# Queueing the last load of v one unit sooner, and a GpSimd drain right after its last store

One core of one Trainium2 chip (trn2). The metric is the device time of one execution in microseconds (us), of which several are taken; the profile is of one execution, and its span starts and ends with the program's first and last instruction, so it is some 1.7 us shorter than the time.

## The reference

```python
attn_weights: float32 [8, 12, 1024, 1024]      v: float32 [8, 12, 1024, 64]
out = np.einsum('bhqs,bhsd->bhqd', attn_weights, v)          # float32
```

There are 96 heads. The kernel takes them two at a time, as 48 units (numbered 0 to 47). A unit's attention is 8 MB in HBM and is cast to bf16 on its way in; the loads of all units are nearly all of the kernel's traffic.

## The kernel before

GpSimd issues every transfer that casts (all attention, all v but the first), and every store but those of the last unit. It does so in one program order, and its transfers run through one queue, in that order. TensorE transposes a unit's attention in 16 groups (line 129), spreads v over the partitions (line 144, waits for v) and multiplies (line 172; in the last three units line 225, group by group). VectorE and ScalarE copy between.

The parts that matter, with cuts marked:

```python
HELD = 9                       # the last nine GpSimd stores wait until all loads are queued
pieces_of = {                  # unit -> pieces of its attention load, (first group, groups)
    NP - 4: [(0, GH), (GH, GH)],
    NP - 3: [(0, GH), (GH, GH)],
    NP - 2: [(0, 4), (4, 4), (8, 4), (12, 4)],
    NP - 1: [(0, 4), (4, 4), (8, 4), (12, 2), (14, 1), (15, 1)],
}
# ... TensorE, units 45 to 47
            transpose_g(abf[i], g)
            if g == 3:
                # ...
                elif p == NP - 2:
                    pe.wait_ge(s_vlast, 16)          # unit 46 needs the last v here
                spread_v(i, vr_of(p))
# ... GpSimd
HELD_FROM = NP - 1 - HELD
for p in range(NP - 2):
    pool.wait_ge(s_t[True], (p + 1) * PER_DVE)       # unit p is transposed: its buffer is free
    if p % 2 == 1 and (p + 1) // 2 < NV:
        iv = (p + 1) // 2
        if iv < NV - 1:
            pool.wait_ge(s_sp[1], p + 1)
        load_v(iv)                                   # iv == NV - 1 goes to vr_last
    load_attn(p + 2)
    if 0 < p <= HELD_FROM:
        store(p - 1)
for p in range(HELD_FROM, NP - 1):
    store(p)
# ... SyncE: the last unit's four stores as they become ready, then waits for all stores
```

`vr_last` is a buffer of its own, used by nothing else, so its load has nothing to wait for. A buffer of attention serves every second unit.

## Time and profile before

| | |
|---|---|
| time, median of 3 runs | 1068.31 us (1067.46 to 1068.49) |
| span of the profiled execution | 1066.0 us |
| loads and stores in GpSimd's queue | 128 |
| last attention piece landed | 1040.9 us |
| GpSimd's last store landed | 1052.2 us |
| last copy of a result by an engine | 1058.0 us |
| SyncE's last store landed | 1059.65 us |

A landing is read as the issue's start plus the latency that the profile gives for that transfer's tile. The page's "chain that ended last" ends with the last instruction of a compute engine; what lies between that and the end of the span (8 us here) is not in it and has to be read from the landings and from the sequencers' instructions. The lines themselves stand in the prediction.

### The profile page before, as it was taken

Reading aid. Unit: us, or ns where it says so; the run is one execution under the profiler, and the core shown is the slowest. Engines: PE = TensorE matmul, PEld = TensorE weight load, DVE = VectorE, ACT = ScalarE, POOL = GpSimd, SP = SyncE. Lnnn points to the kernel's source line nnn. Section 1 sums busy time; section 2 is a strip of 40 time slices with the busy share of each in tenths; the row PEclk is TensorE's granted clock in tenths of the full one; section 3 lists DMA queues with packets and bytes.
Section 4 is the critical chain, followed back from the end, with each engine's and each line's share of the span. In section 5 each row is a group of like instructions: output and inputs, shape, how many; then the busy total and the mean of one; then the engine's idle time right before and its main releaser. Section 6 shows DMA issues by size and latency. Waiting matters only on the chain.

```text
span 1066.0 us, 12832 instructions
## 1 busy us (share of the span) xinstructions
PE 792.5 (74%) x5640; PEld 635.4 (60%) x5640; DVE 391.8 (37%) x589; ACT 397.1 (37%) x485; POOL 71.1 (7%) x137
## 2 busy tenths in 40 slices
PE   0896686867877778768787787767876778769866
PEld 0764575646655666546665575556755566558755
DVE  0443353333433344334343343333433334335423
ACT  0343343333433334333343343333433334335423
POOL 1000000000000000000000000000000000001020
PEclk9898898888989789898888798987889889889979
DMA  9999999999999999999999999999999999999994
GB/s 216 217 217 219 242 225 230 223 229 237 223 231 222 236 230 223 230 231 227 230 224 221 243 223 231 222 229 239 221 231 221 236 232 221 218 215 216 212 217 189
DMA packets 19171, 239.84 MB, mean 225 GB/s; under 512 B 2128, under 2 KB 2512, under 8 KB 11984
## 3 DMA queue, kind: packets, MB, share of 16 engines
q0 software_dynamic: 18432, 238.03, 99.3%
q1 hardware_dynamic: 720, 1.57, 0.4%
q8 instruction: 9, 0.15, 0.0%
q14 instruction: 10, 0.08, 0.0%
HBM read 427.82 MB, written 25.17 MB: 425 GB/s over the span
## 4 chain that ended last, share of the span: by engine, by line
DMA 67%; PE 29%; issue 1%; POOL 1%; ACT 1%; DVE 0%; POOLq 0%; SPq 0%
DMA abf<-in_attn_weights_dram 66%; PE bank L129 23%; PE bank L144 2%; PE bank L225 2%; DMA vr_last<-in_v_dram 1%; POOL vr L387 1%; PE bank L172 1%; ACT at L320 0%; PE bank L156 0%; DVE vbf L295 0%; DVE at L320 0%; DVE osb L307 0%; ACT osb L347 0%; ACT vbf L295 0%; POOL abf L381 0%
## 5 line engine op out<-in xcount | busy, mean ns | idle before, releaser
L129 PE MATMUL bank<-ident,abf 128*128 128x128 f32 x3072 | 464.1, 322 | 251.0 <-DMA abf<-in_attn_weights_dram 251.0
L129 PEld LDWEIGHTS bank<-ident,abf 128*128 128x128 f32 x3072 | 452.1, 215 | 273.3 <-DMA abf<-in_attn_weights_dram 247.7
L320 DVE COPY at<-bank 128x1024 bf16<-128x1024 bf16 x480 | 320.6, 689 | 469.8 <-PE bank L129 465.1
L320 ACT COPY at<-bank 128x1024 bf16<-128x1024 bf16 x288 | 289.0, 1012 | 421.5 <-PE bank L129 421.4
L172 PE MATMUL bank<-at,vbf 128*64 128x512 bf16 x1440 | 216.4, 391 | 0.8 <-DVE vbf L295 0.8
L172 PEld LDWEIGHTS bank<-at,vbf 128*64 128x64 bf16 x1440 | 106.5, 108 | 96.1 <-DVE vbf L295 8.2
L357 ACT COPY ot<-bank 128x512 f32<-128x512 f32 x45 | 26.3, 585 | 183.7 <-PE bank L172 183.7
L357 DVE COPY ot<-bank 128x512 f32<-128x512 f32 x45 | 31.1, 692 | 144.4 <-PE bank L172 144.4
L381 POOL DMA_DIRECT2D abf<-in_attn_weights_dram x58 | 31.0, 539 | 398.2 <-PE bank L129 395.2
L156 PEld LDWEIGHTS bank<-ident,ot 128*128 128x128 f32 x360 | 38.5, 140 | 19.1 <-issue 19.1
L156 PE MATMUL bank<-ident,ot 128*128 128x128 f32 x360 | 49.1, 280 | 0.0
L347 ACT COPY osb<-bank 128x512 f32<-128x512 f32 x90 | 48.3, 589 | 0.4
L144 PE MATMUL bank<-vr,spread 32*128 32x512 bf16 x368 | 48.1, 377 | 0.0
L387 POOL DMA_DIRECT2D vr<-in_v_dram x22 | 11.6, 528 | 476.5 <-PE bank L144 476.5
L295 DVE CAST vbf<-bank 128x512 bf16<-128x512 f32 x48 | 33.2, 692 | 24.6 <-PE bank L144 24.6
L295 ACT CAST vbf<-bank 128x512 bf16<-128x512 f32 x48 | 28.1, 585 | 32.3 <-PE bank L144 32.3
L225 PE MATMUL bank<-vbf,at 128*128 128x128 bf16 x384 | 28.0, 227 | 4.3 <-DVE vbf L295 1.9
L397 POOL DMA_DIRECT2D out_dram<-osb x47 | 25.1, 543 | 70.9 <-ACT osb L347 48.3
L225 PEld LDWEIGHTS bank<-vbf,at 128*128 128x128 bf16 x384 | 24.4, 102 | 7.7 <-issue 3.2
L144 PEld LDWEIGHTS bank<-vr,spread 32*128 32x128 bf16 x368 | 15.4, 93 | 15.7
L307 DVE COPY osb<-bank 64x256 f32<-64x256 f32 (+1 forms) x13 | 5.1, 395 | 22.0 <-PE bank L225 22.0
L307 ACT COPY osb<-bank 64x256 f32<-64x256 f32 (+1 forms) x13 | 4.6, 351 | 22.1 <-PE bank L225 22.1
(13 smaller groups left out, 10.7 us busy)
## 6 DMA issues: line engine op xcount, KB each, us to landing
abf<-in_attn_weights_dram POOLq DMA_DIRECT2D x44, 4096.0 KB, 32.3
out_dram<-osb POOLq DMA_DIRECT2D x47, 512.0 KB, 32.1
vr<-in_v_dram POOLq DMA_DIRECT2D x22, 512.0 KB, 12.7
abf<-in_attn_weights_dram POOLq DMA_DIRECT2D x4, 2048.0 KB, 25.2
abf<-in_attn_weights_dram POOLq DMA_DIRECT2D x7, 1024.0 KB, 24.1
v<-in_v_dram SPq DMA_DIRECT2D x1, 1024.0 KB, 4.8
vr_last<-in_v_dram POOLq DMA_DIRECT2D x1, 512.0 KB, 12.2
abf<-in_attn_weights_dram POOLq DMA_DIRECT2D x1, 512.0 KB, 26.0
```

The source lines that it names most:

```text
L129: last = pe.matmul(out=pt[g % 4][:, k], lhsT=words[:, k], rhs=ident, is_transpose=True, start=(k == 0), stop=(k == KW - 1),)
L144: last = pe.matmul(out=po[h], lhsT=spread[rows, b], rhs=source[rows, b], start=(b == 0), stop=(b == VB - 1),)
L156: last = pe.matmul(out=px[n][:, ds(j * P, P)], lhsT=ot[:, 4 * n + j].rearrange("p h q -> p (h q)"), rhs=ident, is_transpose=True, start=(j ...
L172: last = pe.matmul(out=po[h][ds(half * D, D)], lhsT=vbf[i][:, 2 * kw + par, h], rhs=at[:, ds(half * GH, GH), kw, ds(h * HP, HP), par], sta ...
L225: last = pe.matmul(out=x[:, g - g0], lhsT=at[:, g, kw, :, par], rhs=vbf[i][:, 2 * kw + par].rearrange("p h d -> p (h d)"), start=(n == 0), ...
L295: copy(out=vbf[i][:, :, h], in_=po[h].rearrange("p (k d) -> p k d", k=SB)).then_inc(s_vbf[i][h])
L320: ins = copy(out=at[:, g].rearrange("c k j two -> c (k j two)"), in_=bank[g % 4].bitcast(bf16),)
L347: last = nc.scalar.copy(out=halves[:, :, ds(4 * n, 4)].rearrange("p half j d -> p j half d"), in_=px[n].rearrange("p (j half d) -> p j hal ...
L357: copy(out=ot[:, :, h], in_=po[h].rearrange("p (j q) -> p j q", j=GH)).then_inc(s_ot[p % 2][h])
L381: pool.dma_start(out=abf[p % 2][:, ds(g0, gn)].rearrange("p g s -> p (g s)"), in_=attn_p[p][:, ds(g0 * S, gn * S)],).then_inc(s_piece[p, n ...
L387: pool.dma_start(out=vr_of(2 * iv).rearrange("p b x -> p (b x)"), in_=v_g[iv]).then_inc(s_v if iv < NV - 1 else s_vlast, 16)
L397: pool.dma_start(out=out_p[p].rearrange("p g d -> p (g d)"), in_=osb[p % NO].rearrange("p g d -> p (g d)"), single_packet=True,).then_inc( ...
```

## The change

Two things. The last v has a buffer that is free from the start, so it can be queued before unit 46's attention rather than behind it. And GpSimd drains as soon as its last store is queued, so that the drain in the closing barrier finds nothing left to do. (A drain, `pool.drain()`, is an instruction of GpSimd's own sequencer. The closing barrier is what the trace has at the end on line 480: all engines drain there and wait for each other.)

```diff
         for p in range(NP - 2):
             pool.wait_ge(s_t[True], (p + 1) * PER_DVE)
-            if p % 2 == 1 and (p + 1) // 2 < NV:
-                iv = (p + 1) // 2
-                if iv < NV - 1:
-                    pool.wait_ge(s_sp[1], p + 1)
-                load_v(iv)
+            if p % 2 == 1 and (p + 1) // 2 < NV - 1:
+                pool.wait_ge(s_sp[1], p + 1)
+                load_v((p + 1) // 2)
             load_attn(p + 2)
+            if p == LOOPED - 1:
+                load_v(NV - 1)
             if 0 < p <= HELD_FROM:
                 store(p - 1)
         for p in range(HELD_FROM, NP - 1):
             store(p)
+        pool.drain()
```

## The prediction

> **What bounds the kernel now.** I read the page first, then the stretches of the last 56 us, then the chain that ended last, then the landings of the last transfers, and last the sequencers' own instructions after the final store. On the page, the DMA row says that the transfers, not an engine, carry the kernel:
>
> ```profile
> DMA  9999999999999999999999999999999999999994
> ```
>
> Every fortieth of the span is full except the last. So the change, which touches only the last four of 48 units, can win nothing before about 1008 us; it can win only time in which the DMA engines were not full. The stretches of the end show where that is (columns: stretch, length, busy time of PE, PEld, DVE, ACT, POOL with counts, granted clock, DMA share, GB/s):
>
> ```profile
> 1010.00:1021.00 11.00, 1.84 (x17) 1.65 (x17) 1.60 (x3) 2.15 (x3) 7.35 (x14) 0.68 1.04 216
> 1021.00:1052.00 31.00, 28.94 (x315) 25.95 (x315) 13.98 (x23) 11.43 (x16) 0.54 (x1) 0.89 0.99 282
> 1052.00:1058.00 6.00, 5.47 (x72) 4.98 (x69) 2.87 (x6) 2.91 (x5) 0.00 (x0) 1.00 0.08 27
> 1058.00:1060.00 2.00, 0.00 (x0) 0.00 (x0) 0.00 (x1) 0.00 (x0) 0.00 (x0) 1.00 0.23 66
> 1060.00:1066.00 6.00, 0.00 (x0) 0.00 (x0) 0.00 (x0) 0.00 (x0) 0.00 (x0) 0.65 0.00 0
> ```
>
> Up to 1052 the transfers are full (1.04 and 0.99); from 1052 to 1058 TensorE works alone at a DMA share of 0.08; from 1060 nothing computes or moves. So about 8 us are TensorE finishing late, and 6 us are an ending with nothing in it. The chain says why TensorE is late:
>
> ```profile
> 1008.65 12.21 DMA vr_last<-in_v_dram
> 1020.86 0.05 issue
> 1020.91 1.89 PE bank L144 x7
> 1022.80 0.02 issue
> 1022.83 0.70 DVE vbf L295
> 1023.53 0.20 issue
> 1023.73 3.57 PE bank L225 x32
> ```
>
> GpSimd queues the last v at 1008.65 and it lands 12.21 us later; TensorE sat 9.2 us for it (its idle time before line 144, from the waits). After it the spread took 1.89 us and the first multiplications 3.57; the next unit's took 1.05 and 1.95. Landings, from the tiles, are issue plus latency (minimum / median / maximum): unit 46's four attention pieces, then unit 47's six, then the eight held stores, then the ninth.
>
> ```profile
> L381 POOL DMA_DIRECT2D abf<-in_attn_weights_dram x4: 533/552/567, 982.9 to 984.4; - x4
> DMA to landing us min/median/max: 20.9/27.4/34.0
> ```
> ```profile
> L381 POOL DMA_DIRECT2D abf<-in_attn_weights_dram x6: 535/552/575, 1010.8 to 1013.4; - x6
> DMA to landing us min/median/max: 14.9/25.1/27.5
> ```
> ```profile
> L397 POOL DMA_DIRECT2D out_dram<-osb x1: 538/538/538, 1040.6 to 1040.6; - x1
> DMA to landing us min/median/max: 11.6/11.6/11.6
> ```
>
> Unit 46: first piece at 982.9 + 20.9 = 1003.8, last at 984.4 + 34.0 = 1018.4. The last v follows at 1020.86: 2.5 us of its own transfer, and some 9.7 of its 12.2 us behind unit 46's attention. Unit 47: first at 1010.8 + 14.9 = 1025.7, last at 1013.4 + 27.5 = 1040.9. The ninth store lands at 1052.2, so nine stores took 11.3 us, 1.25 each. Finally, the GpSimd sequencer's own instructions on the line of the kernel's closing barrier:
>
> ```profile
> L480 POOLq EVENT_SEMAPHORE  x4: 17/17/17, 1064.8 to 1065.9; - x4
> L480 POOLq DRAIN  x3: 51/188/4711, 1060.0 to 1065.7; - x3
> ```
>
> Of the 6 us, 4.71 us are one drain of GpSimd, from 1060.0 to 1064.7, though its own last transfer had landed at 1052.2. The two drains after it took 0.19 and 0.05.
>
> **What the Trainium skill says.** "DMA: Bandwidth & Descriptors", section "Two DMAs through the same engine are not ordered": within one queue of a DMA engine, descriptors start in order. The trace agrees: v landed 2.5 us after the last attention piece queued before it. Section "Queues, rings and completion order" of that page: an engine with work on several queues alternates between them by packets; so SyncE's last stores need not wait for GpSimd's backlog, and its first one, issued at 1049.94 into that backlog, did land in 2.9 us. "Perfetto Trace Analysis", section "Sequencer-only Instruction (DRAIN, etc)": a drain's recorded time is its execution, without semaphore waits; so I take the 4.71 us as work or waiting inside GpSimd. No page that I found says what that work is. "TensorE: Matmul & The Clock Gate", section "What's actually happening": an idle window of about 3.4 us halves the array's clock; the trace agrees, with 0.68 granted in the stretch of the 9.2 us stall and 1.89 us for work that takes 1.05 later.
>
> **The change part by part.** The instruction order confirms that the last v moves from behind unit 46's attention to behind unit 45's, and that no instruction on another engine moves.
>
> *The load.* Unit 45's second half lands at 998.9, so v lands at about 998.9 + 2.5 = 1001.4, and unit 46's pieces each 2.5 us later: first 1006.3, last 1020.9. From there the queue has carried the same bytes as before, so unit 47 still lands from 1025.7 to 1040.9. Does TensorE feel the 2.5 us? It reaches unit 46 at 1009.6 in the trace, 3.3 us after the new landing: no. Its path then: transposes of four groups to 1011.75, spread 1.05, about 15 us for the remaining groups of unit 46 (16.7 us in the trace from the spread's end to unit 47, less 1.6 us of the slow clock), so unit 47 begins near 1027.9 instead of 1039.5, which is after its first piece. Unit 47 took 18.5 us from its first transpose to its last copy at 1058.0, so it ends near 1046.4. TensorE gains about 11.6 us.
>
> The end of the kernel does not gain that much, because the stores become the bound. Behind the last attention piece (1040.9) wait nine held stores of 1.25 us and SyncE's four small ones, together the size of one more: 10 x 1.25 = 12.5 us, to about 1053.5. The last store landed at 1059.65 before. So this part is worth 6.2 us, the share of the 11.6 that DMA leaves.
>
> *The drain.* The instruction is added after the ninth store is queued, which will be near 1028 (unit 46's end). SyncE's last wait now ends near 1053.5, and 0.36 us later (1059.65 to 1060.01 in the trace) GpSimd would start its closing drain. If the early one has done the work by then, the closing one costs like the second, 0.19 us: 4.5 us won. The rest of the ending, 1.24 us from 1064.72, stays. Sum: 1053.5 + 0.4 + 0.2 + 1.2 = 1055.3 of span, 10.7 less. The median of 1068.31 less 10.7 is 1057.6.
>
> **The rivals.** (1) The drain is not hidden. If its 4.7 us begin only when the last transfer has landed, then, now that GpSimd's stores and SyncE's end together at 1053.5, it ends near 1058.2 and the ending near 1059.7: 1062.0. If each drain costs the same, the closing one repeats it: 1062.1. For this: in the kernel before it took 4.7 us with every transfer landed for 7.8 us, so it is not plain waiting for data. Against: two more drains within a microsecond took 0.19 and 0.05, so it clears something once. I give this rival 40%. (2) TensorE stays the last to finish, since some other wait takes the place of v's. It has some 7 us of slack (1046.4 against 1053.5), so this needs an error of 7 us; worst case is the old end less the drain, 1063.8. 5%. (3) Unit 46's attention, 2.5 us later, stalls TensorE: 3.3 us of slack against it, and what it costs falls in TensorE's slack; no change of the time. (4) The drain disturbs the transfers or the queue; nothing in the trace speaks for it, and it comes after the last issue.
>
> **Range and chances.** All outcomes are gains of 4 to 11 us on 1068, 0.4 to 1.0%; 2% would need 21 us, more than the whole stretch after 1052 with nothing in flight. Before's three runs spread by 1.0 us. I lean to the hidden drain, but shade towards the rival: 1058.7, from 1056.0 to 1063.0; faster by 2% 0.01, slower 0.01.
>
> **What would show it.** TensorE's stall before line 144 in unit 46 gone and its granted clock near full there; unit 47's last piece still near 1041; DMA share near 1 to about 1053 and GpSimd's last store, not TensorE, ending last; a short closing drain. A 4.7 us closing drain, or an early drain that ends several us after the last landing, proves rival 1. A last copy by TensorE's chain after 1053 proves rival 2. The forecast fails if unit 47's landings move.

## The result, and the profile after

| | before | after |
|---|---|---|
| time, median of 4 runs of each | 1067.95 us | 1059.62 us |
| ratio | | 0.9922 (0.9905 to 0.9939) |
| span of the profiled execution | 1066.0 | 1057.9 |
| last copy of a result | 1058.0 | 1046.2 |
| last store landed | 1059.65 (SyncE's) | 1054.1 (GpSimd's) |
| from there to the end of the span | 6.35 | 3.8 |

The gain is 0.8%, but clear of noise: no run of one kernel overlaps the other's. Of the 8.1 us of span, 5.5 come from the earlier last landing and 2.6 from the shorter ending.

The stretches of the changed kernel's end (stretch, length, busy time of PE, PEld, DVE, ACT, POOL with counts, granted clock, DMA share, GB/s):

```profile
1010.00:1021.00 11.00, 9.98 (x115) 8.97 (x114) 5.75 (x10) 4.78 (x8) 7.35 (x14) 1.00 1.03 216
1021.00:1046.20 25.20, 23.51 (x285) 21.67 (x284) 12.64 (x22) 11.66 (x17) 0.54 (x1) 1.00 1.03 271
1046.20:1050.50 4.30, 0.00 (x0) 0.00 (x0) 0.00 (x0) 0.00 (x0) 0.00 (x0) 0.72 1.04 413
1050.50:1054.20 3.70, 0.00 (x0) 0.00 (x0) 0.00 (x0) 0.00 (x0) 0.00 (x0) 0.50 0.29 113
1054.20:1057.90 3.70, 0.00 (x0) 0.00 (x0) 0.00 (x0) 0.00 (x0) 0.00 (x0) 0.50 0.00 0
```

TensorE is busy 9.98 of the 11 us in which it had been busy for 1.84, at full granted clock. The picture has turned round: now the engines are finished at 1046.2 and the transfers go on without them, full to 1050.5, then at a share of 0.29. The chain of the changed kernel at the place of the old stall and at its end (start, length, what):

```profile
1009.71 1.99 PE bank L129 x16
1011.70 0.98 PE bank L144 x7
1012.67 0.02 issue
1012.70 0.70 DVE vbf L295
1013.40 0.29 issue
1013.69 1.95 PE bank L225 x32
...
1027.83 1.99 PE bank L129 x16
...
1045.90 0.28 DVE osb L307
```

No transfer stands between the transposes and the spread (line 144) any more; the multiplication takes 1.95 instead of 3.57. The chain ends at 1046.2, although the span goes on for 11.7 us: it has nothing to say about what now sets the time. That is in the landings of the last v, of unit 46's four pieces, of unit 47's six, and of the ninth held store:

```profile
L387 POOL DMA_DIRECT2D vr_last<-in_v_dram x1: 557/557/557, 971.0 to 971.0; - x1
DMA to landing us min/median/max: 30.3/30.3/30.3
...
L381 POOL DMA_DIRECT2D abf<-in_attn_weights_dram x4: 532/552/567, 982.8 to 984.4; - x4
DMA to landing us min/median/max: 23.3/29.9/36.9
...
L381 POOL DMA_DIRECT2D abf<-in_attn_weights_dram x6: 537/552/575, 1010.4 to 1013.0; - x6
DMA to landing us min/median/max: 15.7/25.4/27.9
...
L397 POOL DMA_DIRECT2D out_dram<-osb x1: 538/538/538, 1028.8 to 1028.8; - x1
DMA to landing us min/median/max: 25.3/25.3/25.3
```

v lands at 1001.3 with a latency of 30 us that hurts nobody; unit 46 from 1006.1 to 1021.3; unit 47 from 1026.1 to 1040.9, where it had landed before; the ninth store at 1054.1. Last, GpSimd's drains in the changed kernel: the early one (line 440) and those of the closing barrier (line 481):

```profile
L440 POOLq DRAIN  x1: 27720/27720/27720, 1028.8 to 1028.8; - x1
```
```profile
L481 POOLq DRAIN  x3: 39/47/188, 1056.6 to 1057.6; - x3
```

The first closing drain is down from 4711 ns to 47. But the early one, which begins at 1028.8, ends at 1028.77 + 27.72 = 1056.49, that is 2.37 us after the last store landed, and only then does the closing barrier pass.

### The profile page after: what moved, and what is told of

The parts are those of the page before. It is cut to its first block, busy times and chain, and to the rows that moved or that the text cites. A ratio compares the mean times of both kernels' runs of the same rounds, so it can differ in the third digit from the quotient of the medians.

```text
span 1057.9 us, 12833 instructions
## 1 busy us (share of the span) xinstructions
PE 791.0 (75%) x5640; PEld 634.7 (60%) x5640; DVE 391.8 (37%) x589; ACT 397.3 (38%) x485; POOL 71.0 (7%) x137
## 4 chain that ended last, share of the span: by engine, by line
DMA 66%; PE 29%; issue 1%; POOL 1%; ACT 1%; DVE 0%; POOLq 0%; SPq 0%
DMA abf<-in_attn_weights_dram 66%; PE bank L129 23%; PE bank L144 2%; PE bank L225 2%; POOL vr L387 1%; PE bank L172 1%; ACT at L320 0%; PE bank L156 0%; DVE vbf L295 0%; DVE at L320 0%; DVE osb L307 0%; ACT osb L347 0%; ACT vbf L295 0%; POOL abf L381 0%; POOLq L431 0%
## 5 line engine op out<-in xcount | busy, mean ns | idle before, releaser
L387 POOL DMA_DIRECT2D vr<-in_v_dram x22 | 11.6, 527 | 474.0 <-PE bank L144 474.0
```

The costliest lines, as they stand in the source:

```text
L387: pool.dma_start(out=vr_of(2 * iv).rearrange("p b x -> p (b x)"), in_=v_g[iv]).then_inc(s_v if iv < NV - 1 else s_vlast, 16)
```

## The experiments

The theory at this point: the end is set by the transfers, then by the part of the drain that cannot lie beside them. The rivals: TensorE still sets the end; or the drain contributes nothing; or it waits for all transfers of the core. Unless said otherwise all runs gave the right result.

**The changed kernel again**, as the measure on the chip of the next three.

> The changed kernel again, on the chip of the runs beside it: about 1059.6 us, last store landed near 1054.1 and the early drain ending about 2.4 us after it. All theories expect the same here; it is the measure for the others.

Measured 1059.52 us (1059.20 to 1059.81), against 1068.06 for before on the same chip; ratio 0.992.

**Only the earlier load.**

```diff
         for p in range(HELD_FROM, NP - 1):
             store(p)
-        pool.drain()
```

> Only the earlier load of v, no early drain. Theory (parts add up to the end of the transfers plus a drain): stores end near 1054.1 as in the changed kernel, the closing drain takes the full 4.7 us there, span about 1060.5, time about 1062.3, that is 5.5 to 6 us less than before. Rival (the closing drain is shorter when less time has passed, or overlaps the last landings): time below 1061. Rival (the early drain won everything): time as before, 1068.

Measured 1062.26 us (1062.07 to 1062.31), 5.8 less than before; ratio 0.9946. The drains of its closing barrier:

```profile
L480 POOLq DRAIN  x3: 51/188/4711, 1054.5 to 1060.1; - x3
```

The closing drain takes exactly what it took before, 4711 ns, though now it starts 0.4 us after the last landing instead of 7.8 us after GpSimd's last one. So the time is not a matter of how long ago the transfers landed. The theory holds; both rivals fall.

**Only the drain**, in the order of before.

```diff
         for p in range(HELD_FROM, NP - 1):
             store(p)
+        pool.drain()
```

> Only the early drain, v late as before. Theory: GpSimd's own last store lands at 1052.2 and the drain ends about 2.4 us later, near 1054.6, in the shadow of TensorE, which ends at 1058 and SyncE's last landing at 1059.65; the closing drain takes 0.05 us instead of 4.71. Span about 1061.3, time about 1063.1, 4.7 us less than before. Rival (every drain costs 4.7): time as before. Sum of the two parts alone 10.2 to 10.7 us, against 8.3 measured together.

Measured 1063.60 us (1063.08 to 1064.05), 4.5 less than before; ratio 0.9958. The early drain of this kernel, and those of its closing barrier:

```profile
L440 POOLq DRAIN  x1: 13712/13712/13712, 1040.9 to 1040.9; - x1
```
```profile
L481 POOLq DRAIN  x3: 39/47/188, 1060.3 to 1061.6; - x3
```

It ends at 1054.6, again 2.4 us after GpSimd's last store (issued at 1040.9, landed 11.3 us later), but here TensorE and SyncE go on to 1060, so all of it is hidden. The two parts alone give 5.8 + 4.5 = 10.3 us, together 8.5 on this chip. The 1.7 us between (5.80 + 4.46 - 8.54) are the price of doing both: once the load is early, GpSimd's last store is the last thing to land, and the drain's remainder has nothing left to hide behind.

**v behind the third of unit 46's pieces**: how much slack has TensorE?

```diff
 # in load_attn, after each piece is queued
+                if p == NP - 2 and n == 2:
+                    load_v(NV - 1)
 # in GpSimd's loop
-            if p == LOOPED - 1:
-                load_v(NV - 1)
```

> The changed kernel with the last v queued behind the third of unit 46's four attention pieces: it lands near 1016.0 instead of 1001.3. Theory (the end is set by the transfers, TensorE has some 6 to 8 us of slack): TensorE stalls about 4.3 us before its spread and ends unit 47 near 1051 instead of 1046, the stores still end near 1054, time within 0.5 us of the changed kernel (1059.6). Rival (the end is set by TensorE): about 4 to 6 us later, near 1064.

Measured 1059.14 us (1058.63 to 1059.47), against 1067.72 for before on its chip; ratio 0.9919. TensorE did stall, by the waits of this kernel (who, by what: us, times, longest), and its last copies came at 1052.3 instead of 1045.9 (VectorE's is shown, ScalarE's starts with it):

```profile
PE bank L144 <- DMA vr_last<-in_v_dram: 4.1, 1, 4.1
```
```profile
1052.30 0.28 DVE L307 COPY osb<-bank 64x128 f32<-64x128 f32 x1 [0.53 <-PE bank L225]
```

Six us later at TensorE's end, no loss in the time: TensorE does not set the end of the changed kernel. It has some 6 us of slack: about half of the 12 us that its end moved forward was not needed for the gain. (With v this late, SyncE's last store lands at 1054.4, 0.7 us after GpSimd's. The early drain still ends last, at 1056.1, so a little more slack may be left.)

**The held stores by SyncE**: does the drain wait for GpSimd's own transfers only, and can the remainder be hidden?

```diff
         def store(p, eng):              # eng instead of pool throughout
-            ).then_inc(s_osb[p % NO], 16)
+            ).then_inc(s_osb[p % NO] if p < HELD_FROM else s_held, 16)
 # GpSimd
-        for p in range(HELD_FROM, NP - 1):
-            store(p)
         pool.drain()
 # SyncE, ahead of the last unit's stores
+        nc.sync.wait_ge(s_piece[NP - 1, 3], 16)
+        for p in range(HELD_FROM, NP - 1):
+            store(p, nc.sync)
```

(SyncE's closing waits follow the semaphores.)

> The changed kernel with the nine held stores issued by SyncE once the fourth attention piece of the last unit has landed, instead of by GpSimd. Theory (the drain waits for GpSimd's own transfers plus about 2.4 us): GpSimd's last transfer now lands near 1041 and its drain ends near 1043 to 1046; the ending after the last landing shrinks from 3.8 us to about 1.7 us. If the bytes still end near 1054, span about 1055.8, time about 1057.5, 2 us less than the changed kernel. Rival (the drain waits for all transfers of the core, or costs the same at the close): no gain. Rival (stores issued by SyncE run slower or leave a gap at the hand-over): gain eaten by a later last landing.

Measured 1058.02 us (1057.72 to 1058.13); ratio to before 0.9906. On the same chip the changed kernel had 1059.20 to 1059.81, so this is 1.5 us faster than it, with no overlap of runs. Its early drain, its last loads, SyncE's last four stores (the latencies are of all thirteen; the last store took 3.0), and the closing drains:

```profile
L439 POOLq DRAIN  x1: 30477/30477/30477, 1012.7 to 1012.7; - x1
```
```profile
L381 POOL DMA_DIRECT2D abf<-in_attn_weights_dram x6: 542/562/585, 1010.5 to 1013.1; - x6
DMA to landing us min/median/max: 15.8/25.5/28.0
```
```profile
L452 SPq DMA_DIRECT2D out_dram<-osb x4: 667/1074/1190, 1047.9 to 1051.5; - x4
DMA to landing us min/median/max: 2.9/5.2/6.5
```
```profile
L484 POOLq DRAIN  x3: 39/47/195, 1054.9 to 1056.1; - x3
```

The drain ends at 1012.66 + 30.48 = 1043.1, 2.0 us after GpSimd's last load landed at 1041.1, while SyncE's stores ran on to 1054.5. So it waits for GpSimd's own transfers and for no others. The ending after the last landing is 1.9 us instead of 3.8; the last landing itself came 0.4 us later than in the changed kernel, which is what the gain lacks of the expected 2.

**The same, and the last unit's stores by ScalarE**, beside a repeat of the one above on the same chip.

```diff
 # ScalarE, after its copy of a group that ends one of the last unit's stores
+                    for s in (s_od, s_oa):
+                        eng.wait_ge(s, k + 1)
                     # ... (gs: the groups of that store)
+                    eng.dma_start(out=out_p[p][:, gs], in_=osb[p % NO][:, gs]).then_inc(s_end, 16)
 # ... SyncE's own loop over these four stores is taken out
```

> The version with SyncE's held stores again, on the chip of the next one: about 1058.0 us, last landing near 1054.5.

> As that version, but the last unit's four stores are issued by ScalarE, on its own queue, so that they don't stand behind the held ones in SyncE's. Theory (engines take turns between queues): they land by about 1052 instead of 1054.5 and the end is set by the held stores, near 1053.5; time about 1057.0, 1 us less than with SyncE alone. Rival (only the bytes count): no change, 1058.0. Rival (ScalarE's issuing delays its copies): later.

Measured 1057.95 us (1057.92 to 1058.05) with SyncE alone, 1057.78 (1057.53 to 1057.91) with ScalarE: ratios 0.9907 and 0.9905. The runs of the two do not overlap, but by 0.01 us and with four of each, so the 0.2 us is not surely told apart from nothing. ScalarE's four stores did land sooner, by 1052.2 instead of 1054.3, but the held ones then ended at 1054.2 instead of 1053.0. The theory's 1 us is not there; what the one queue gained the other lost.

**What is the drain's work?** Four probes put drains behind chosen sets of transfers, each set landed and waited for beforehand, in a program made slower on purpose (their times mean nothing). The diff is of the first; its comments stand for code that is cut here. In all of them the first drain follows the kernel's own 128 transfers.

```diff
         for p in range(HELD_FROM, NP - 1):
             store(p)
+        # wait until all stores have landed
         pool.drain()
+        pool.drain()
+        # then 1, 2, 4, 8 stores; 8 with a wait after each; 1 and 8 of a sixteenth of the size;
+        # each set waited for, and a pool.drain(); 8 and 1 stores without a wait, and a pool.drain()
```

> A probe, slower on purpose: after all of its transfers have landed, GpSimd drains; again at once; then repeats stores (the same data to the same places) and drains after 1, 2, 4, 8 of them have landed, after 8 issued one by one, after 1 and 8 of a sixteenth of the size, and twice without waiting for the landing (8 and 1 stores). Theory A (bookkeeping for each transfer not yet settled): near 0.5 us for one, rising by about 0.47 us a store, 4 us for 8; less for 8 one by one if issuing settles earlier ones. Theory B (a fixed walk, for instance over the DMA engines): about 4.7 us for 1, 2, 4 and 8 alike, and 0.05 to 0.2 only when nothing was issued since. Theory C (work by bytes or descriptors): the small ones cost a fraction of the large ones. Without waiting for the landing: the drain ends 2.4 us after the last landing if part of the work overlaps the transfers.

The drains of the first probe, each from the answer for its own line (duration in ns, minimum/median/maximum of the one):

```profile
L461 POOLq DRAIN  x1: 4714/4714/4714, 1054.2 to 1054.2; - x1
L462 POOLq DRAIN  x1: 40/40/40, 1059.0 to 1059.0; - x1
L464 POOLq DRAIN  x1: 129/129/129, 1062.4 to 1062.4; - x1
L466 POOLq DRAIN  x1: 203/203/203, 1067.4 to 1067.4; - x1
L468 POOLq DRAIN  x1: 371/371/371, 1075.1 to 1075.1; - x1
L470 POOLq DRAIN  x1: 691/691/691, 1088.4 to 1088.4; - x1
L472 POOLq DRAIN  x1: 691/691/691, 1114.8 to 1114.8; - x1
L474 POOLq DRAIN  x1: 119/119/119, 1117.8 to 1117.8; - x1
L476 POOLq DRAIN  x1: 697/697/697, 1123.8 to 1123.8; - x1
L478 POOLq DRAIN  x1: 9688/9688/9688, 1128.1 to 1128.1; - x1
L481 POOLq DRAIN  x1: 2987/2987/2987, 1138.3 to 1138.3; - x1
```

Read from the top: the first settles the kernel's transfers, 4.71 us; the one at once after it has nothing to do, 0.04. Then 1, 2, 4 and 8 stores: 0.13, 0.20, 0.37, 0.69, a straight line of about 0.08 us a store. Eight issued one by one cost the same as eight together (both 691), and a sixteenth of the bytes, in 32 packets instead of 144, costs the same (119 and 697). So it is work for each transfer since the last drain, whatever its size, after it has landed: theory A in kind, though a store costs 0.08 us and not 0.47. Theories B and C fall. Without waiting (line 478), the drain ended at 1137.83 and the last of the eight landed at 1137.47: 0.36 us after it, half of the 0.69. In the changed kernel it was 2.37 of 4.71, again half; with SyncE's stores (119 transfers instead of 128) 2.0; for the single store of line 481, 0.08 of 0.13. So about half of the work can lie beside the transfers and half comes after the last landing; what the halves are no run shows.

That leaves a riddle: at 0.08 us each, 128 transfers should cost 10 us, not 4.71. The first of three further probes drained after 16, 32, 48, 56, 64 and 96 small stores.

> A second probe, slower on purpose: after a drain that settles everything, 16, 32, 48, 56, 64 and 96 small stores with a drain after each set, everything landed before each drain. From the first probe: 0.047 us and 0.0805 us for each transfer, so 1.34, 2.62, 3.91 and 4.56 us for 16 to 56. Theory A (only as many transfers as some list holds are left unsettled, and the full list costs 4.7 us): 4.7 us at 64 and at 96 alike, as after the kernel's own 128 transfers. Theory B (no such limit; the kernel's loads cost less than stores): 5.2 and 7.8 us.

Three of its six drains (after 16, 64 and 96):

```profile
L466 POOLq DRAIN  x1: 1354/1354/1354, 1070.7 to 1070.7; - x1
...
L466 POOLq DRAIN  x1: 5264/5264/5264, 1227.5 to 1227.5; - x1
L466 POOLq DRAIN  x1: 7877/7877/7877, 1301.9 to 1301.9; - x1
```

(7.877 - 1.354) / 80 = 0.0815 us each, without a limit up to 96; a list that is full at about 58 does not exist. By this line 4.71 us is the price of 57 transfers.

The next probe asked whether loads cost less.

> A third probe, slower on purpose: after a drain that settles everything, 16 casting loads of v (0.5 MB each), 16 casting loads of a quarter unit of attention (1 MB), 8 of a whole unit (4 MB), each set landed and then drained; at last 64 small stores and 64 loads of v, 128 in all as in the kernel. The second probe gave 0.0815 us a store without a limit up to 96, so 128 would be 10.5 us, but the kernel's 128 (47 stores, 81 loads) took 4.71. Theory L (loads cost less: 4.66 less 47 x 0.0815 leaves 0.83 us for 81 loads, 0.010 us each): 0.21 us for 16 loads, 5.9 us at the end. Theory W (a load costs as much as a store, and something before the end of the kernel had settled some 70 of them): 1.35 us for 16, 0.70 for 8, and 10.5 or less at the end.

Sixteen loads of v cost 1.349 us, sixteen of a quarter unit 1.344, eight of a whole unit (eight times as large as v's) 0.691: a load costs what a store costs, so theory L falls. And 64 stores followed by 64 loads cost the price of 64:

```profile
L482 POOLq DRAIN  x1: 5264/5264/5264, 1835.1 to 1835.1; - x1
```

So part of the transfers had been settled before the drain. The last probe varied the mixture.

> A fourth probe, slower on purpose: after a drain that settles everything, 128 small stores; 32 stores then 32 loads; 64 loads then 64 stores; 32 store-load pairs; 48 stores then 80 loads; each set landed, then a drain. 64 stores then 64 loads cost 5.264 us in the third probe, the price of 64. Theory P (stores and loads are settled side by side, the larger number sets the time): 10.5, 2.65, 5.26, 2.65, 6.6 us. Theory C (a transfer costs 0.0815 us whatever its kind, and a list of limited length between 96 and 128 is emptied at issue when it is full): 64-transfer sets 5.26 us, the 128-transfer sets all much under 10.5, near 4 to 6.

Its drains, after 128 stores; 32 stores and 32 loads; 64 loads and 64 stores; 32 pairs; 48 stores and 80 loads:

```profile
L474 POOLq DRAIN  x1: 1267/1267/1267, 1153.8 to 1153.8; - x1
L478 POOLq DRAIN  x1: 5264/5264/5264, 1347.4 to 1347.4; - x1
L482 POOLq DRAIN  x1: 5264/5264/5264, 1737.8 to 1737.8; - x1
L486 POOLq DRAIN  x1: 5264/5264/5264, 1978.1 to 1978.1; - x1
L490 POOLq DRAIN  x1: 6571/6571/6571, 2441.5 to 2441.5; - x1
```

The two sets of 64 in all cost the price of 64, so stores and loads are not settled side by side and theory P falls. 128 stores cost the price of 15, so 113 had been settled before the drain. That is in the direction of theory C for this set, but when and where they were settled the run does not show. In the mixtures of 128, what is left is 64 of 64 + 64 and the 80 loads of 48 + 80, as if the older kind were settled as a block; that reading fits four sets but was not tested by itself. The kernel's own 57 of 128 fits somewhere between and stays open: what settles 71 of its transfers early was not found. With the nine held stores on SyncE the part after the landing was 0.37 us shorter (2.37 to 2.00), nine halves of 0.0815, so by this estimate the nine are among the 57.

## Why the prediction was right, point by point

The prediction (1058.7, range 1056.0 to 1063.0) held: 1059.62 measured. That the number came within 0.9 us is in part luck: its own sum gave 1057.6, rival 1 gave 1062.0, and 1058.7 was a hedge between the two. The measured time lies between them because half of the drain was hidden, a case that it did not name. By its steps:

- *The stall goes, and the later landing of unit 46 hurts nobody.* Right: first piece at 1006.1 (1006.3 predicted), unit 47's last at 1040.9 (the same), clock full.
- *TensorE gains 11.6 us and ends near 1046.4.* Right: 1046.2.
- *The stores become the bound; the end gains less than TensorE.* Right, and shown by moving v: six us of TensorE's gain given back, no loss. The term "10 x 1.25 = 12.5 us" was a little small: 13.2 measured, from 1040.9 to 1054.1, and 5.5 us won instead of 6.2. In the last 3.7 of them the DMA share was 0.29; whether a few DMA engines lagged or all of them had pauses was not looked into.
- *The drain is hidden, 4.5 us won.* This is the term that was mis-sized: 2.6 us. Neither the full success nor rival 1 came true, but half of each: half of the drain's work ran beside the transfers, and half, 2.37 us, came after the last landing. The prediction saw that GpSimd's stores and the kernel's last landing would come together, but priced only all or nothing for what follows. Had the working been for the drain alone, 4.5 us would have been right (4.5 measured).
- *Rival 2* (TensorE last) and *rival 4* (the drain disturbs transfers) did not show: the last landing was at 1054.1 with the early drain and without it; rival 3 was harmless, as argued.
- *A store of SyncE need not wait for GpSimd's backlog.* Not so for the first: 6.2 us to landing instead of 2.9. The 2.9 us were a poor test of it, since GpSimd's queue was running empty: it took 0.25 of the DMA engines' time from 1050.50 to 1050.75, and SyncE's first packet moved at 1050.8. It is off the path (SyncE's stores landed by 1052.4), and is told below.

## What to carry to other kernels

Work in the shadow of a stall is cheap only while the stall lasts: two gains that were measured alone, 5.8 and 4.5 us, give 8.5 together, since the first takes away what hides the second. When a transfer has a buffer of its own, place it in the queue by when its data is needed, not by when its turn comes in the loop: the wait was for what stood ahead of it in the queue. And if an engine that issued many transfers must settle them at the end, let another engine issue the last ones, so that the settling lies beside them: that version ran at 1058.0 us, 1.5 us less than the changed kernel on the same chip.

## What the Trainium skill lacked or had wrong

- **A GpSimd drain costs time for each transfer that GpSimd issued since its last drain** (no page that I found has this cost): 0.04 us with none, 0.0815 us for each, load or store, 32 KB or 4 MB alike if it has landed, up to 96 in a row. Of 128 in a row, 15 to 80 were left to pay for; this kernel's end takes 4.71 us. The drain waits for GpSimd's own transfers, and about half of its work comes after the last landing (2.37 of 4.71, 0.36 of 0.69).
- **"VectorE: DVE Perf Modes", section "The DRAIN you can't avoid"**, gives the runtime's own drains, of the preamble and postamble, as about 12 ns, constant, on all five engines. VectorE's two in the closing barrier here take 10 ns, but GpSimd's take 39 to 188 ns, and 4711 in the kernel before. Whether the page means these too, which the trace puts on a line of the kernel, it does not say.
- **"Perfetto Trace Analysis", section "Sequencer-only Instruction (DRAIN, etc)"**: the recorded time leaves out waits on semaphores. That it includes, for a GpSimd drain, the wait for the transfers is not said there: 27.7 us in the changed kernel.
- **"DMA: Bandwidth & Descriptors", section "Queues, rings and completion order"**: the alternation between queues did show, but late, and the section gives no such delay. A store that SyncE issued at 1038.1 in the changed kernel moved its first packet 3.5 us later. From 1038.5 to 1041.0 the trace has packets of GpSimd's queue alone (a share of 105.2%), and from 1041.5 to 1043.0 of both (65.7% and 35.0%). The last attention piece landed at 1040.9, but that is not what the store waited for. In the run with v behind the third piece the same store was issued 3.7 us after that landing, and its first packet again came 3.4 us later; it landed 5.8 us after its issue at 1044.5. Where GpSimd's queue was about to run empty (before, and with the held stores on SyncE) the first packet came after 0.8 us. What sets the 3.4 us no run was made to find.
